# Layer 0's down projection: F tiles 16 to 21 of both token chunks by seven block products in place of eight

## The chip, the cores and the metric

The kernel runs on one core of a Trainium2 chip. The metric is the device time of one execution in microseconds (us), the median over several runs. The core's engines are TensorE (PE in the profile, its weight loads PEld), VectorE (DVE), ScalarE (ACT), GpSimd (POOL) and SyncE (SP). SP and POOL also issue the DMAs; each works off its queue in order.

## The reference

Two residual layers over 1024 tokens of width 1024, each a token mixer (layer 0 a causal convolution module, layer 1 a multi-scale pooling) and a SwiGLU network with 2816 hidden channels:

```python
def swiglu_ffn(h, w_gate, w_up, w_down):
    return (jax.nn.silu(h @ w_gate) * (h @ w_up)) @ w_down
...
for i in range(DEPTH):
    mod = c_act @ ada_w[i] + ada_b[i]
    sh_m, sc_m, g_m, sh_f, sc_f, g_f = jnp.split(mod, N_ADA, axis=-1)
    h = modulate(rms_norm(x, norm_mix_g[i]), sh_m, sc_m)
    y = conformer_conv(h, ...) if i % 2 == 0 else multiscale_pool(h, ...)
    x = x + (1.0 + g_m)[:, None, :] * y
    h = modulate(rms_norm(x, norm_ffn_g[i]), sh_f, sc_f)
    x = x + (1.0 + g_f)[:, None, :] * swiglu_ffn(h, ...)
return rms_norm(x, final_g)
```

The change is in `@ w_down` of layer 0: the hidden values g (2816 by 1024 tokens) times a 2816 by 1024 matrix.

## The kernel before

**Tiles.** Tokens are two chunks, A and B, of 512. Channels lie on the 128 partitions: 8 blocks d of the model width, 22 F tiles of the hidden width, two to a pair. A float32 operand is split into a high part (a copy on ScalarE, `hi` or the first half of `w`) and a low part (a subtraction on VectorE, `lo` or the second half). `products` (line 505) issues three 128x512 matmuls for each product of a weight tile and an operand: a row "x3" of PE's order is one product.

**Stages, in PE's order.** Layer 0's convolution; `heads` (gate and up of chunk A's first pairs, and their part of A's down); `joint` (gate and up of the rest for both chunks together, in fewer products by a block scheme on sums and differences); `downs` (line 1860), first of chunk A's remaining F tiles, then of all 22 of chunk B; then the same for layer 1. A gated tile g goes to DRAM (`gd`) and comes back when its down is due.

**Down** (`down`, line 1404). F tiles are taken in groups of up to four (`fours`); for each of eight output blocks d the group's products add up in one of the `dn` banks, and `update` (line 1021) has VectorE add the bank, times a gain, to `x`. A's 14 remaining tiles make four groups, B's 22 make six.

**Layer 1's down** already goes by `Seven` (line 1504): four F tiles are taken as a 2 by 2 block of matrices over the two halves of the output and the two tokens' chunks, and p1 to p7 (seven products of sums of weight blocks `wds` and of operands `kinds`, `kept`) replace eight. Each such product is added to up to two places of `x`, so its bank is read by VectorE once for each place, and p1, p6, p7, p4 go on adding to one set of four banks, with reads between. Weights are combined by a load that adds to a tile already loaded (`plus` in `weights_of`, line 1441: an SP load, then a POOL load with addition) and by subtraction on VectorE.

**The pool mixer of chunk A** (layer 1's first part) is done beside B's down of layer 0. `pool_start(A)` (line 1942) puts a task with VectorE's work in the planner's list: A's norm statistics (`acc`, a matmul `var` over 128 channels, eight small steps to the reciprocal root, a matmul `rstd` that spreads it), then `t`, the window sums `win` and their difference to the token, whose low parts are the rows `mx<-win`. `pool_end(A)` (line 1947) puts the mixer's 16 products (`y<-mx`, 48 matmuls), with the rest of the task ahead of them, at a place in PE's order.

**What sets the order.** PE's order is as the program emits it (`manual_schedule`, line 134). While it emits, `pace` (line 233) keeps a clock for each engine from the costs in `PRICES` (line 93) and lets the tasks on VectorE go ahead up to 4 us past PE's clock; a task that waits for another engine is held back for a `DELAY`. So where a row stands in VectorE's queue is decided by these planned clocks. VectorE works its queue strictly in order. Other work that it has here: low parts of weights (`w<-raw`), dot products of layer 1's conditioning (`adaw`, 128x1024, each with a 512 KB load on POOL's queue) and the updates (`x<-dn`).

Of the kernel before, what the change touches and what calls it, by code (L numbers as in the profile page):

```python
# [9 lines left out]
F32 = mybir.dt.float32  # L10
# [46 lines left out]
ON_DVE = (1, 4)  # L57
AHEAD = 4
RECENT = 6
STRASSEN = (False, True)  # L60
NQ = -(-NP // 2)
LAST = (2, 3, 4)
LOADED = 4
SPLIT = 2
# [67 lines left out]
def trunk(ctx, tc, xT, c, vec, ada, adan, w1f, w1, wdg, w2, wgu, wdn, wds, wpl, out):  # L132
# [72 lines left out]
    def nm(s):  # L205
        uid[0] += 1
        return f"{s}_{uid[0]}"
# [131 lines left out]
    rd = [[dram.tile([P, 2, 512], F32, name=f"rd_{l}_{f}") for f in range(NP)] for l in range(DEPTH)]  # L339


    kept_d = [[dram.tile([P, 2, 512], F32, name=f"kept_{l}_{q}") for q in range(NQ)] if STRASSEN[l] else [] for l in range(DEPTH)]
    kinds_d = [[[dram.tile([P, 2, 2, 512], F32, name=f"kinds_{l}_{q}_{b}") for b in range(3)] for q in range(NQ)] if STRASSEN[l] else [] for l in range(DEPTH)]
    KINDS = {"t1": (0, 0), "b22": (0, 1), "t3": (1, 0), "t2": (1, 1), "b11": (2, 0), "t4": (2, 1)}

    def x_out(ch):
# [693 lines left out]
    def gated(l, i, f, g, u, kept=False, into=None):  # L1040

        t = temp(512)
        S_.activation(t, g, AF.Silu)
        if into is not None:
            V_.tensor_tensor(into, u, t, op=MUL)
            return
        V_.tensor_tensor(t, u, t, op=MUL)
        if STRASSEN[l]:
            soft.dma_start(kept_d[l][f // 4][:, f // 2 % 2], t)
            if not kept:  # L1050
                return
        both = block("u0", "g")
        split(t, both, V_ if kept else None)
        if kept:
            st["g", i, f] = both[:, 0], both[:, 1]
        else:
            soft.dma_start(gd[l][i][f], both.bitcast(F32))
# [60 lines left out]
    def joint_weights(l, fp):  # L1118

        w = {}  # L1120

        def added(i, src):
            d = order(nc.gpsimd.dma_start(w[i], wgu[l, fp, src], accum_op=ADD))  # L1123
            if fp == 1:
                st["added"].append(d.ins)
            clock["G"] = max(clock["G"], clock["PE"]) + 0.9

        def loads():
            for i in (0, 3, 2, 1) if fp else (2, 0, 3, 1):
                w[i] = quarter(l, fp, i, "u1")  # L1130
            if fp == 2:
                V_.tensor_tensor(w[0], w[0], w[2], op=ADD)
            elif fp == 1 and l == 0:
                V_.tensor_tensor(w[0], w[0], w[2], op=ADD)
                if st["third"]:
                    tc.add_manual_dep(V_.last.ins, st["third"], edge, reason="behind the combinations")
                else:
                    st["early"].append(V_.last.ins)
            else:
                added(*((0, 2) if fp else (2, 3)))  # L1140
            added(*((2, 3) if fp else (0, 2)))

        def later():

            if fp == 1 and st["read"]:
                tc.add_manual_dep(V_.last.ins, st["read"], edge, reason="behind the first unit's reads")
            elif fp == 1:
                st["next"].append(V_.last.ins)

        def s2():  # L1150
            if fp:
                loads()
            w[4] = block("u0", "s2", F32).rearrange("p a b -> p (a b)")
            either(D).tensor_tensor(w[4], w[0], w[3], op=ADD)
            later()
            wt = combined(w[4])
            later()
            return wt

        def s1():  # L1160
            if fp == 0:
                loads()
            wt = combined(w[2], fp == 0)
            if fp:
                later()
            return wt

        def s3():
            wt = combined(w[0], fp == 0, True)
            later()  # L1170
            return wt

        def s4():
            either(D).tensor_tensor(w[1], w[1], w[4], op=ADD)
            if STRASSEN[l] and "taken" in st:
                tc.add_manual_dep(V_.last.ins, st["taken"], edge, reason="behind the second sum's banks")
            return combined(w[1])

        def a22():
            wt = combined(w[3], fp == 0 and l == 0, True, wgu[l, fp, 3])  # L1180
            if fp == 0 and l == 0:
                return wt
            if fp == 0 and st["third"]:
                tc.add_manual_dep(V_.last.ins, st["third"], edge, reason="behind the combinations")
            elif fp == 0:
                st["early"].append(V_.last.ins)
            return wt

        return s2, s1, s3, s4, a22

    def joint(l, fp, between=None):
# [29 lines left out]
        def after5(o, b):  # L1221
            if fp:
                r = temp(512)
            else:
                c["r15"] = c["r15"] if o else block("u0", "r15", F32)
                r = c["r15"][:, o]
            c["r15", o] = r
            V_.tensor_tensor(r, b, c["r1"][o], op=ADD)
            if STRASSEN[l] and o:
                st["taken"] = V_.last.ins.name  # L1230

        def ended(r, i, f, op):
            def after(o, b):
                t = c["r1"][o] if r == "r1" else c[r, o]
                V_.tensor_tensor(t, b, t, op=op)
                c["c", o] = t
                if fp == 0 and r == "r15" and o:
                    st["read"] = V_.last.ins.name
                    for ins in st["next"]:
                        tc.add_manual_dep(ins, st["read"], edge, reason="behind the first unit's reads")  # L1240
                if o and STRASSEN[l]:
                    paired(i, f, c["c", 0], t)
                elif o:
                    gated(l, i, f, c["c", 0], t)
            return after
# [195 lines left out]
    def weights_of(l, kind, q, placed=True):  # L1441

        n = duo_width(q) * 512
        src = lambda b: wds[q, b][:, :n]
        got = {}

        def behind_products(d):
            if placed:
                tc.add_manual_dep(d.ins, last_mm[0], held_by if kind == "s4" else edge, reason="behind the products")

        def plus(r, what):
            behind_products(nc.gpsimd.dma_start(r, what, accum_op=ADD))
            clock["G"] = max(clock["G"], clock["PE"]) + 0.9

        def load():
            if kind == "a11":
                st["sum", q] = block("h1", "s", F32).rearrange("p a b -> p (a b)")[:, :n]
            if kind in ("a11", "s2", "s4"):
                r = st["sum", q]
            else:  # L1460
                r = (raw_tile() if placed else raws.tile([P, D], F32, tag="raw", name=nm("raw")))[:, :n]
            first = {"a11": 0, "a12": 1, "a22": 3, "s1": 2, "s3": 3}.get(kind)
            if first is not None:
                behind_products(nc.sync.dma_start(r, src(first)))
            if kind in ("s1", "s4"):
                plus(r, src(3 if kind == "s1" else 1))
            got["raw"] = r

        def halves():
            r = got["raw"]  # L1470
            if kind == "s3":
                V_.tensor_tensor(r, r, st["sum", q], op=ADD)
            wt = wts.tile([P, 2, D], F32R, tag="w", name=nm("w"))
            S_.copy(wt[:, 0, :n], r)
            V_.tensor_tensor(wt[:, 1, :n], r, wt[:, 0, :n].bitcast(F32), op=SUB)
            if kind == "s1":
                st["then_sum"] = lambda: V_.tensor_tensor(st["sum", q], st["sum", q], r, op=SUB)
            return wt

        return load, halves  # L1480
# [85 lines left out]
    def one_half(l, qs):  # L1566
# [14 lines left out]
        bs = []  # L1581
        for q in qs:
            unit(emit_of(q, bs), lambda q=q: queued(weights_of(l, "a12", q, False)))

    def ending(ch, l):

# [284 lines left out]
    def heads(l, n, first):  # L1871

        for r in range(ROUNDS[l]):
            fps = range(r * ROUND, (r + 1) * ROUND)
            in_turn(l, fps, True)
            if r == 0:
                first()
            if STRASSEN[l]:
                one_half(l, [fps[0] // 2, fps[0] // 2 + 1])
            else:  # L1880
                down(A, l, [2 * q for q in fps])
# [7 lines left out]
    def all_joint(l, n, first=None, behind_it=None, between=None):  # L1889
# [3 lines left out]
        unit(lambda take: T.__setitem__("comb", Task(combinations(l, st["sq"]), True)))  # L1893
        in_turn(l, range(n, NP), behind_it=behind_it)
        need("comb")
        rest = [2 * q for q in range(ROUNDS[l] * ROUND, NP)] + list(range(1, NF, 2))
        for fp in range(NP):
            joint(l, fp, between if fp == NP - 1 else None)
            if 2 < fp <= 2 + KT // 2:
# [1 line left out]
            if fp == 0:  # L1901
                if first is not None:
                    first()
            if fp == NP - 2 and not STRASSEN[l]:
                unit(fetch(A, l, fours(rest)[0], "h1"))
        return rest

# [28 lines left out]
        for k in range(KT):  # L1936
            yield from pool_mixed(ch, k)

    downs(A, 0, rest, "h1", {0: lambda: unit(lambda take: x_in(B))}, True)
    unit(lambda take: lax.__setitem__(0, True))  # L1940

    def pool_start(ch):
# [13 lines left out]
        else:  # L1956
            unit(lambda take: st.__setitem__("sq", sq[0]))

    downs(B, 0, list(range(NF)), "h1", {0: lambda: pool_start(A), 4: lambda: pool_end(A)})
    need("norm_a")  # L1960
    pool_start(B)
    heads(1, HEADS[1], lambda: None)
# [88 lines left out]
```

## Time and profile before

| what | value |
|---|---|
| median of 3 runs | 1693.41 us (1692.5 to 1693.59) |
| the profiled execution | 1691.56 us, its span 1689.7 us |
| mean granted TensorE clock | 0.998 |
| PE busy | 1663.7 us, 98% of the span |
| DVE busy | 1318.1 us, 78% |
| ACT, POOL busy | 798.4 us (47%), 490.9 us (29%) |
| DMA | 380.71 MB, mean 225 GB/s |

Time outside the span is 1.86 us. PE is busy nearly all the time, so a matmul less is time saved unless PE is then made to wait; a wait of PE is time lost. Times in the views are microseconds from the start of the span. An instruction's duration overlaps the next one's on the same engine a little: how far apart instructions start is the better measure of what each costs in a row.

### The profile page before, as it was taken

Reading aid. Unit: us, or ns where it says so; the run is one execution under the profiler, and the core shown is the slowest. Engines: PE = TensorE matmul, PEld = TensorE weight load, DVE = VectorE, ACT = ScalarE, POOL = GpSimd, SP = SyncE. Lnnn points to the kernel's source line nnn. Section 1 sums busy time; section 2 is a strip of 40 time slices with the busy share of each in tenths; the row PEclk is TensorE's granted clock in tenths of the full one; section 3 lists DMA queues with packets and bytes.
Section 4 is the critical chain, followed back from the end, with each engine's and each line's share of the span. In section 5 each row is a group of like instructions: output and inputs, shape, how many; then the busy total and the mean of one; then the engine's idle time right before and its main releaser. Section 6 shows DMA issues by size and latency. Waiting matters only on the chain.

```text
span 1689.7 us, 21273 instructions
## 1 busy us (share of the span) xinstructions
PE 1663.7 (98%) x7586; PEld 1357.1 (80%) x7586; DVE 1318.1 (78%) x1872; ACT 798.4 (47%) x1085; POOL 490.9 (29%) x566
## 2 busy tenths in 40 slices
PE   6999999999999999999999999999999999999997
PEld 5777777778888888888888888888888888888887
DVE  8889899899759888887665797848777777668656
ACT  3669686867546332333213336646422222234344
POOL 3587767797001121221110221100111111000013
PEclk9999999999999999999999999999999999999999
DMA  7957997828677788886877846877677776577564
GB/s 288 296 181 221 226 240 209 225 77 237 206 243 177 257 262 300 280 268 208 338 267 269 262 147 201 241 244 212 178 231 218 225 220 192 205 268 208 191 168 125
DMA packets 115885, 380.71 MB, mean 225 GB/s; under 512 B 12289, under 2 KB 14465, under 8 KB 115778
## 3 DMA queue, kind: packets, MB, share of 16 engines
q1 hardware_dynamic: 78464, 247.99, 41.4%
q0 software_dynamic: 36736, 130.83, 31.7%
q8 instruction: 60, 0.98, 0.2%
q10 hardware_dynamic: 578, 0.53, 0.1%
q14 instruction: 47, 0.39, 0.1%
HBM read 311.92 MB, written 63.18 MB: 222 GB/s over the span
## 4 chain that ended last, share of the span: by engine, by line
PE 90%; DVE 4%; DMA 2%; issue 1%; POOL 1%; ACT 1%; SPq 0%; DVEq 0%; ACTq 0%; POOLq 0%
PE a L149 25%; PE dn L149 23%; PE e L149 14%; PE p L149 12%; PE y L149 6%; PE g L149 3%; PE first L149 3%; PE tap L149 2%; POOL pa L126 1%; PE ada L149 1%; DMA adaw<-in_adan_dram 1%; DVE t L126 1%; PE var L149 1%; DVE x L126 1%; DVE ca L126 0%
## 5 line engine op out<-in xcount | busy, mean ns | idle before, releaser
L126 ACT CAST w<-raw 128x1024 fp32r<-128x1024 f32 (+1 forms) x249 | 258.6, 1041 | 324.8 <-PE dn L149 92.1
L149 PE MATMUL dn<-g,w 128*128 128x512 f32 x1152 | 265.4, 391 | 1.7 <-DVE g L126 1.0
L149 PEld LDWEIGHTS dn<-g,w 128*128 128x128 f32 x1152 | 215.5, 188 | 48.0 <-DVE g L126 1.3
L126 DVE TENSOR_TENSOR w<-raw,w 128x1024 fp32r<-128x1024 f32 (+1 forms) x177 | 217.7, 1232 | 38.2 <-ACT w L126 37.8
L149 PE MATMUL a<-n,w 128*128 128x512 f32 x1056 | 246.9, 390 | 0.2
L149 PE MATMUL p<-h,w 128*128 128x512 f32 x1056 | 244.2, 391 | 0.8 <-DVE h L126 0.7
L126 POOL TENSOR_TENSOR pa<-pa,pr 128x512 f32<-128x512 f32 x160 | 228.2, 1510 | 23.7 <-ACT pr L126 17.5
L149 PEld LDWEIGHTS p<-h,w 128*128 128x128 f32 x1056 | 197.3, 188 | 43.8 <-DVE h L126 1.5
L149 PEld LDWEIGHTS a<-n,w 128*128 128x128 f32 x1056 | 198.2, 188 | 42.1 <-DVE r L126 1.1
L149 PE MATMUL dn<-hi,w 128*128 128x512 f32 (+1 forms) x600 | 173.9, 373 | 0.5 <-DVE w L126 0.5
L126 DVE SCALAR_TENSOR_TENSOR ca<-u,vecs,ca 128x512 f32<-128x512 f32 x245 | 169.6, 745 | 0.5
L126 DVE SCALAR_TENSOR_TENSOR x<-dn,gains,x 128x512 f32<-128x512 f32 (+1 forms) x144 | 100.7, 729 | 35.4 <-PE dn L149 35.1
L149 PEld LDWEIGHTS dn<-hi,w 128*128 128x128 f32 x600 | 109.8, 188 | 20.6 <-DVE w L126 1.0
L149 PE MATMUL a<-t,w 128*128 128x512 f32 x528 | 123.3, 389 | 0.0
L149 PE MATMUL e<-b,w 128*128 128x512 f32 x528 | 123.3, 389 | 0.0
L149 PE MATMUL e<-t,w 128*128 128x512 f32 x528 | 123.3, 389 | 0.0
L126 ACT ACTIVATE pr<-u,vecs 128x512 f32<-128x512 f32 x160 | 108.3, 717 | 25.3 <-POOL pa L126 17.6
L1123 POOL DMA_DIRECT2D raw<-in_wgu_dram x41 | 36.2, 882 | 275.2 <-DVE k L126 106.9
L149 PEld LDWEIGHTS a<-t,w 128*128 128x128 f32 x528 | 99.1, 188 | 20.6
L149 PEld LDWEIGHTS e<-b,w 128*128 128x128 f32 x528 | 99.1, 188 | 20.5
L149 PEld LDWEIGHTS e<-t,w 128*128 128x128 f32 x528 | 99.1, 188 | 20.5
L149 PE MATMUL dn<-lo,w 128*128 128x512 f32 (+1 forms) x300 | 111.7, 372 | 0.0
(183 smaller groups left out, 2376.1 us busy)
## 6 DMA issues: line engine op xcount, KB each, us to landing
raw<-in_wgu_dram SPq DMA_DIRECT2D x132, 512.0 KB, 4.8
adaw<-in_ada_dram POOLq DMA_DIRECT2D x48, 512.0 KB, 7.3
raw<-in_wdn_dram SPq DMA_DIRECT2D x44, 512.0 KB, 7.7
raw<-in_wgu_dram POOLq DMA_DIRECT2D x41, 512.0 KB, 7.5
raw<-in_w_dram SPq DMA_DIRECT2D x36, 512.0 KB, 5.7
gd<-g POOLq DMA_DIRECT2D x36, 512.0 KB, 8.2
g<-gd SPq DMA_DIRECT2D x36, 512.0 KB, 5.4
kinds<-k POOLq DMA_DIRECT2D x33, 512.0 KB, 7.3
```

The lines of the kernel that those rows point to most:

```text
L126: self.last = self.order(getattr(self.eng, name)(out, *args, **kw))
L149: last_mm[0] = nc.tensor.matmul(out, lhsT, rhs, start=start, stop=stop, skip_group_check=more).ins.name
L1123: d = order(nc.gpsimd.dma_start(w[i], wgu[l, fp, src], accum_op=ADD))
```

## The change

F tiles 16 to 21 of layer 0's down are taken by seven products, as `q=4` (tiles 16 to 19) and `q=5` (tiles 20 and 21, half the width). A's remaining tiles are then 8 (two groups), followed by p2, p1, p6, p7, p4, p5, p3, each for q=5 and q=4; p4 completes chunk A. Then come B's first 16 tiles (four groups in place of six). `pool_start(A)` moves behind p4, `pool_end(A)` behind the third of B's groups (before: started behind the first, ended behind the fifth). The hidden values of these tiles go to DRAM as sums (`kinds`, `kept`) and not as `gd`, weights combined in `weights_of` have an own way for layer 0 (s1 is loaded again by an SP and a POOL load, since `s2` comes first).

```diff
-STRASSEN = (False, True)
+BEGINS = (8, 0)
+BY_SEVEN = tuple(range(q, NQ) for q in (BEGINS[0] // 2, 0))
...
-        if STRASSEN[l]:
+        if f // 2 >= BEGINS[l]:
             soft.dma_start(kept_d[l][f // 4][:, f // 2 % 2], t)
...
-            if kind in ("a11", "s2", "s4"):
+            if kind in ("a11", "s2", "s4") and (l or kind != "s2"):
                 r = st["sum", q]
...
-            first = {"a11": 0, "a12": 1, "a22": 3, "s1": 2, "s3": 3}.get(kind)
+            first = {"a11": 0, "a12": 1, "a22": 3, "s1": 2, "s3": 3, **({} if l else {"s2": 2})}.get(kind)
             if first is not None:
                 behind_products(nc.sync.dma_start(r, src(first)))
-            if kind in ("s1", "s4"):
-                plus(r, src(3 if kind == "s1" else 1))
+            if kind in ("s1", "s4") or kind == "s2" and not l:
+                plus(r, src(1 if kind == "s4" else 3))
...
+            elif kind == "s2" and not l:
+                total = st["sum", q]
+                V_.tensor_tensor(total, total, r, op=SUB)
+                r = total
...
+    def seven_queued(l, steps, after):
+
+        todo = [(name, wkind, key, fresh, ends, q) for name, wkind, _, key, fresh, ends in steps for q in BY_SEVEN[l][::-1]]
+        parts = [operand(l, kind, q) for _, _, kind, *_ in steps for q in BY_SEVEN[l][::-1]]
+        last_q, counts, ready, banks = BY_SEVEN[l][0], [0, 0], {}, {}
+
+        def prepare(i):
+            while counts[0] < min(i + LOADED, len(parts)):
+                parts[counts[0]][0]()
+                counts[0] += 1
+            while counts[1] < min(i + SPLIT, len(parts)):
+                ready[counts[1]] = parts[counts[1]][1]()
+                counts[1] += 1
+
+        def emit_of(i, name, wkind, key, fresh, ends, q):
+            def emit(take):
+                wt = take()
+                prepare(i + 1)
+                if fresh and q != last_q:
+                    banks[key] = [bank("dn") for _ in range(4)]
+                bs, ops = banks[key], ready.pop(i)
+                for ds in ((0, 1), (2, 3)):
+                    for j, g in enumerate(ops):
+                        for d in ds:
+                            last = q == last_q and j == len(ops) - 1
+                            products(bs[d], wt, 4 * j + d, g, fresh and q != last_q and j == 0, last, more=True)
+                            if last:
+                                for ch, half in ends:
+                                    update(ch, 4 * half + d, bs[d], gate_f, l)
+                        pace()
+            return emit
...
-        rest = [2 * q for q in range(ROUNDS[l] * ROUND, NP)] + list(range(1, NF, 2))
+        rest = list(range(1, 2 * BEGINS[l], 2))
...
-    downs(B, 0, list(range(NF)), "h1", {0: lambda: pool_start(A), 4: lambda: pool_end(A)})
+    first_b = list(range(2 * BEGINS[0]))
+    begun.append(seven_queued(0, [
+        ("p2", "a12", "b21", "y", True, [(A, 0)]),
+        ("p1", "a11", "b11", "x", True, [(A, 0)]),
+        ("p6", "s2", "t2", "x", False, [(B, 0)]),
+        ("p7", "s3", "t3", "x", False, [(B, 1)]),
+        ("p4", "a22", "t4", "x", False, [(A, 1)]),
+        ("p5", "s1", "t1", "y", True, [(B, 1), (B, 0)]),
+        ("p3", "s4", "b22", "y", True, [(B, 0)]),
+    ], {"p4": lambda: pool_start(A), "p5": lambda: unit(fetch(B, 0, fours(first_b)[0], "h1"))}))
+    downs(B, 0, first_b, "h1", {2: lambda: pool_end(A)}, True)
```

Three places of the instruction order matter below. In an order row the numbers behind the names tell buffers apart. The first place is PE's queue around the pool norm and the pool mixer's products. Before, `var` is row 1318 and the first `y` row 1414, with 94 rows of `dn` and one of `rstd` between:

```order
L149 MATMUL dn_7890<-g_7670,w_7596 128x512 x3
L149 MATMUL dn_7891<-g_7670,w_7596 128x512 x3
L149 MATMUL var_7903<-ones,acc_7773 128x1 x4
L149 MATMUL dn_7890<-g_7672,w_7719 128x512 x3
L149 MATMUL dn_7891<-g_7672,w_7719 128x512 x3
...
L149 MATMUL dn_8416<-g_8223,w_8301 128x512 x3
L149 MATMUL dn_8417<-g_8223,w_8301 128x512 x3
L149 MATMUL y_8465<-mx_8025,w_8314 128x512 x3
L149 MATMUL y_8465<-mx_8033,w_8314 128x512 x3
```

In the changed kernel `var` is row 1492 and the first `y` row 1562, with 68 rows of `dn` and one of `rstd` between; the last pool tile, `mx_8451`, is first used in row 1575:

```order
L150 MATMUL dn_7961<-g_7818,w_7838 128x512 x3
L150 MATMUL dn_7962<-g_7818,w_7838 128x512 x3
L150 MATMUL dn_7989<-g_7812,w_7719 128x512 x3
L150 MATMUL dn_7990<-g_7812,w_7719 128x512 x3
L150 MATMUL dn_7989<-g_7814,w_7768 128x512 x3
L150 MATMUL dn_7990<-g_7814,w_7768 128x512 x3
L150 MATMUL var_8013<-ones,acc_7735 128x1 x4
L150 MATMUL dn_7989<-g_7816,w_7809 128x512 x3
...
L150 MATMUL dn_8397<-g_8172,w_8254 128x512 x3
L150 MATMUL y_8454<-mx_8124,w_8267 128x512 x3
...
L150 MATMUL y_8524<-mx_8451,w_8406 128x512 x3
```

So 26 products (78 matmuls) less stand between `var` and the first `y`: 204 `dn` matmuls in place of 282.

The second place is VectorE's queue at the end of the same stretch. Before, the row of the last low part (`mx_8351<-win`) stands ahead of the first update from `y`:

```order
L126 SCALAR_TENSOR_TENSOR win_8291<-win_8290,hp_7764 128x497
L126 SCALAR_TENSOR_TENSOR x_7217<-dn_8416,gains,x_7217 128x512
L126 SCALAR_TENSOR_TENSOR x_7217<-dn_8417,gains,x_7217 128x512
L126 TENSOR_TENSOR w_8449<-raw_8447,w_8449 128x1024
L126 TENSOR_TENSOR mx_8351<-win_8291,mx_8351 128x512
L126 SCALAR_TENSOR_TENSOR x_5638<-y_8465,gains,x_5638 128x512
```

In the changed kernel the last three low parts come behind updates that read the first `y` banks:

```order
L127 TENSOR_TENSOR mx_8326<-win_8306,mx_8326 128x512
L127 TENSOR_TENSOR win_8329<-win_8330 128x520
L127 TENSOR_TENSOR acc_8462<-acc_8462,t_8494 128x512
L127 TENSOR_TENSOR win_8385<-hp_7726 128x526
L127 TENSOR_TENSOR win_8330<-win_8329 128x512
L127 SCALAR_TENSOR_TENSOR x_6050<-y_8502,gains,x_6050 128x512
...
L127 TENSOR_TENSOR mx_8376<-win_8330,mx_8376 128x512
L127 TENSOR_TENSOR acc_8462<-acc_8462,t_8521 128x512
L127 TENSOR_TENSOR win_8386<-win_8385 128x512
L127 SCALAR_TENSOR_TENSOR win_8386<-win_8386,hp_7726 128x497
L127 TENSOR_TENSOR mx_8451<-win_8386,mx_8451 128x512
```

From the first row on `var` to the last low part these are 95 rows before and 97 in the changed kernel.

The third place is VectorE's queue in the seven products, which before has no counterpart. The banks `dn_7463` to `dn_7466` are those that p1, p6, p7 and p4 share; the updates of `x_7212` and `x_7214` read them behind p6, those of `x_7216` and `x_7218` behind p7; `raw_7611` is s1 of q=4 and `raw_7587` that of q=5:

```order
L127 SCALAR_TENSOR_TENSOR x_7212<-dn_7464,gains,x_7212 128x512
L127 SCALAR_TENSOR_TENSOR x_7214<-dn_7465,gains,x_7214 128x512
L127 SCALAR_TENSOR_TENSOR x_7214<-dn_7466,gains,x_7214 128x512
L127 TENSOR_TENSOR lo_7620<-op_7550,hi_7619 128x1024
L127 TENSOR_TENSOR w_7590<-raw_7587,w_7590 128x512
L127 TENSOR_TENSOR lo_7661<-op_7593,hi_7660 128x512
L127 SCALAR_TENSOR_TENSOR x_7216<-dn_7463,gains,x_7216 128x512
L127 SCALAR_TENSOR_TENSOR x_7216<-dn_7464,gains,x_7216 128x512
L127 SCALAR_TENSOR_TENSOR x_7218<-dn_7465,gains,x_7218 128x512
L127 TENSOR_TENSOR w_7614<-raw_7611,w_7614 128x1024
L127 SCALAR_TENSOR_TENSOR x_7218<-dn_7466,gains,x_7218 128x512
```

The low part of s1's weights now stands ahead of the last of the updates that p4's products wait for.

More of the change, by code (lines that the diff above doesn't have):

```diff
@@ L339, in trunk @@
     rd = [[dram.tile([P, 2, 512], F32, name=f"rd_{l}_{f}") for f in range(NP)] for l in range(DEPTH)]
-    kept_d = [[dram.tile([P, 2, 512], F32, name=f"kept_{l}_{q}") for q in range(NQ)] if STRASSEN[l] else [] for l in range(DEPTH)]
-    kinds_d = [[[dram.tile([P, 2, 2, 512], F32, name=f"kinds_{l}_{q}_{b}") for b in range(3)] for q in range(NQ)] if STRASSEN[l] else [] for l in range(DEPTH)]
+    kept_d = [{q: dram.tile([P, 2, 512], F32, name=f"kept_{l}_{q}") for q in BY_SEVEN[l]} for l in range(DEPTH)]
+    kinds_d = [{q: [dram.tile([P, 2, 2, 512], F32, name=f"kinds_{l}_{q}_{b}") for b in range(3)] for q in BY_SEVEN[l]} for l in range(DEPTH)]
     KINDS = {"t1": (0, 0), "b22": (0, 1), "t3": (1, 0), "t2": (1, 1), "b11": (2, 0), "t4": (2, 1)}
@@ L1174, in s4 @@
             either(D).tensor_tensor(w[1], w[1], w[4], op=ADD)
-            if STRASSEN[l] and "taken" in st:
+            if fp >= BEGINS[l] and "taken" in st:
                 tc.add_manual_dep(V_.last.ins, st["taken"], edge, reason="behind the second sum's banks")
@@ L1228, in after5 @@
             V_.tensor_tensor(r, b, c["r1"][o], op=ADD)
-            if STRASSEN[l] and o:
+            if fp >= BEGINS[l] and o:
                 st["taken"] = V_.last.ins.name
@@ L1240, in after @@
                         tc.add_manual_dep(ins, st["read"], edge, reason="behind the first unit's reads")
-                if o and STRASSEN[l]:
+                if o and fp >= BEGINS[l]:
                     paired(i, f, c["c", 0], t)
@@ L1443, in weights_of @@
         n = duo_width(q) * 512
-        src = lambda b: wds[q, b][:, :n]
+        src = lambda b: wds[l, q, b][:, :n]
         got = {}
@@ L1475, in halves @@
             V_.tensor_tensor(wt[:, 1, :n], r, wt[:, 0, :n].bitcast(F32), op=SUB)
-            if kind == "s1":
+            if kind == "s1" and l:
                 st["then_sum"] = lambda: V_.tensor_tensor(st["sum", q], st["sum", q], r, op=SUB)
@@ L1583, in one_half @@
             unit(emit_of(q, bs), lambda q=q: queued(weights_of(l, "a12", q, False)))
+    def seven_queued(l, steps, after):
[26 more added lines that the diff above has]
+            return emit
+        for i, (name, wkind, key, fresh, ends, q) in enumerate(todo):
+            unit(emit_of(i, name, wkind, key, fresh, ends, q), lambda wkind=wkind, q=q: queued(weights_of(l, wkind, q, False)))
+            if name in after and q == last_q:
+                after[name]()
+        return lambda take: prepare(0)
     def ending(ch, l):
@@ L1877, in heads @@
                 first()
-            if STRASSEN[l]:
+            if not BEGINS[l]:
                 one_half(l, [fps[0] // 2, fps[0] // 2 + 1])
@@ L1903, in all_joint @@
                     first()
-            if fp == NP - 2 and not STRASSEN[l]:
+            if fp == NP - 2 and BEGINS[l]:
                 unit(fetch(A, l, fours(rest)[0], "h1"))
@@ L1937, in pool @@
             yield from pool_mixed(ch, k)
-    downs(A, 0, rest, "h1", {0: lambda: unit(lambda take: x_in(B))}, True)
+    begun = []
+    downs(A, 0, rest, "h1", {0: lambda: (unit(lambda take: x_in(B)), unit(lambda take: begun[0](take)))}, True)
     unit(lambda take: lax.__setitem__(0, True))
@@ L2018 @@
             diag[i, range(P), q, range(P)] = taps[j, p]
-    down = np.asarray(ffn_w_down)[1].reshape(NP, 2, P, 2, D // 2)
-    pairs = np.zeros((NQ, 4, P, 2, D // 2), np.float32)
+    down = np.asarray(ffn_w_down).reshape(DEPTH, NP, 2, P, 2, D // 2)
+    pairs = np.zeros((DEPTH, NQ, 4, P, 2, D // 2), np.float32)
     for q in range(NP):
         for b, (f, half) in enumerate(((1, 0), (0, 0), (1, 1), (0, 1))):
-            pairs[q // 2, b, :, q % 2] = down[q, f, :, half]
-    pairs = pairs.reshape(NQ, 4, P, D)
+            pairs[:, q // 2, b, :, q % 2] = down[:, q, f, :, half]
+    pairs = pairs.reshape(DEPTH, NQ, 4, P, D)
     arrays = {
```

## The prediction

> **What bounds the kernel now.** I read the page first (span, busy time of the engines, chain), then PE's waits, then PE's timeline from the last `joint` products to layer 1's gate, then the windows of that stretch, VectorE's timeline in it and the DMA issues.
>
> ```profile
> span 1689.7 us, 21273 instructions
> PE 1663.7 (98%) x7586; PEld 1357.1 (80%) x7586; DVE 1318.1 (78%) x1872; ACT 798.4 (47%) x1085; POOL 490.9 (29%) x566
> PE 90%; DVE 4%; DMA 2%; issue 1%; POOL 1%; ACT 1%; SPq 0%; DVEq 0%; ACTq 0%; POOLq 0%
> ```
>
> PE is the bound: 98% busy and 90% of the chain. Its waits (kind, total, times, longest) are small:
>
> ```profile
> PE var L149 <- DVE acc L126: 6.5, 1, 6.5
> ...
> PE dn L149 <- DVE g L126: 1.0, 1, 1.0
> ```
>
> The 6.5 us are at the start of the program; no `dn` group of waits is over 1.0 us. So every matmul taken out is time saved, as long as nobody makes PE wait. PE's timeline (start, length, operation, count, idle time before it) around the change:
>
> ```profile
> 811.45 5.60 PE L149 MATMUL e<-b,w 128*128 128x512 f32 x24
> 816.88 5.60 PE L149 MATMUL a<-n,w 128*128 128x512 f32 x24
> 822.33 115.76 PE L149 MATMUL dn<-g,w 128*128 128x512 f32 x510
> 937.92 0.95 PE L149 MATMUL var<-ones,acc 128*128 128x1 f32 x8
> 938.73 4.33 PE L149 MATMUL dn<-g,w 128*128 128x512 f32 x18
> 942.90 0.60 PE L157 MATMUL rstd<-ident,col 128*128 128x128 f32 x4
> 943.26 18.63 PE L149 MATMUL dn<-g,w 128*128 128x512 f32 x81
> 962.14 42.05 PE L149 MATMUL dn<-g,w 128*128 128x512 f32 x183 [0.25 <-DVE x L126]
> 1004.03 11.04 PE L149 MATMUL y<-mx,w 128*128 128x512 f32 x48
> 1014.91 5.60 PE L149 MATMUL dn<-g,w 128*128 128x512 f32 x24
> ```
>
> From 822 to 1015 PE waits once, for 0.25 us. A matmul costs (816.88 - 811.45) / 24, or 0.226 us; over the 48 `y` it is 10.88 / 48 = 0.2267, which I use. VectorE is the other full engine there (window, then its length, PE, PEld, DVE, ACT, POOL busy with counts, clock, DMA share, GB/s):
>
> ```profile
> 822.30:862.00 39.70, 39.70 (x177) 32.87 (x176) 26.18 (x36) 9.06 (x9) 3.98 (x8) 1.00 0.79 297
> 938.00:1004.00 66.00, 65.75 (x295) 53.89 (x294) 59.95 (x95) 25.85 (x33) 19.16 (x30) 1.00 0.65 215
> ```
>
> Beside the pool mixer VectorE is busy 59.95 of 66 us. That is the narrow place.
>
> **Part 1: matmuls removed.** By the instruction order PE has 36 128x512 matmuls less (six F tiles by two chunks by eight blocks are 96 products; seven eighths are 84, so 12 x 3 matmuls go) and no other change of kind. All stand in the dense stretch: 36 x 0.2267 = 8.2 us saved.
>
> **Part 2: the seven products' own stage.** It is 252 matmuls (57 us). One set of banks is read by VectorE and added to again four times in a row, so each product waits for the updates of the one before. VectorE's costs, by the distance between starts:
>
> ```profile
> 938.91 0.16 DVE L126 TENSOR_SCALAR col<-var 128x4 int32<-128x4 int32 x1 [1.39 <-PE var L149]
> 939.11 0.17 DVE L126 TENSOR_TENSOR var<-var,col 128x4 f32<-128x4 f32 x1
> ...
> 940.42 1.23 DVE L126 TENSOR_TENSOR w<-raw,w 128x1024 fp32r<-128x1024 f32 x1
> 941.57 1.22 DVE L126 SCALAR_TENSOR_TENSOR adaw<-adaw,cact 128x1024 f32<-128x1024 f32 x1
> 942.71 0.08 DVE L126 DVE_READ_ACCUMULATOR adaw<-adaw,cact 128x1 f32 x1
> ...
> 950.76 0.68 DVE L126 TENSOR_TENSOR win<-hp 128x512 f32<-128x512 f32 x1
> 951.36 0.74 DVE L126 SCALAR_TENSOR_TENSOR t<-x,gains,ny 128x512 f32<-128x512 f32 x1
> 952.02 0.68 DVE L126 TENSOR_TENSOR win<-hp 128x512 f32<-128x512 f32 x1
> ```
>
> So 1.14 us for 1024 elements (`w`, `adaw`), 0.66 for an update or `t`, 0.60 for other rows of 512, 0.20 for the small steps. The narrow place is s1's weights, which now take two loads one behind the other, SP's and then POOL's adding one (in layer 1's down: landing times):
>
> ```profile
> raw<-in_wds_dram SPq DMA_DIRECT2D x10, 512.0 KB, 7.1
> raw<-in_wds_dram POOLq DMA_DIRECT2D x5, 512.0 KB, 8.1
> ...
> raw<-in_wds_dram SPq DMA_DIRECT2D x5, 512.0 KB, 5.1
> s<-in_wds_dram POOLq DMA_DIRECT2D x5, 512.0 KB, 5.2
> ```
>
> ```profile
> L126 ACT CAST w<-raw 128x1024 fp32r<-128x1024 f32 (+1 forms) x249 | 258.6, 1041 | 324.8 <-PE dn L149 92.1
> L1123 POOL DMA_DIRECT2D raw<-in_wgu_dram x41 | 36.2, 882 | 275.2 <-DVE k L126 106.9
> ```
>
> The SP load reuses a buffer that VectorE frees when it has split a22. That is behind the last of p1's updates: matmul 72 of the stage (16.3 us), an update (0.7), then four rows (1.14 + 1.14 + 1.14 + 0.60), 21.1 us. The chain adds 5.1 to 7.1 (SP), 0.9 (POOL's issue), 5.2 to 8.1 (POOL), 1.04 (ScalarE's copy) and 1.14 (low part): 34.5 to 39.4, and 0.66 for the update queued behind it, 35.2 to 40.1. The fourth bank's product of p4, which needs that update, comes at matmul 153, 34.7 us. PE waits 0.5 to 5.4 us; I take 3, the middle, since the rows come from two stretches with about equal claim. Queued behind: on ScalarE the casts of p5's and p3's operands, on SP B's second weight tile, which has 20 us more before PE needs it; on POOL the clearing of the pool's borders and the first `wdn` load. None of these is due before p4. The operand splits (7 of 1.14, 7 of 0.60) and the subtractions for s2, s3 lie beside 57 us of products, and B's updates are no more than before.
>
> **Part 3: the pool mixer of A.** It moves into a shorter piece of PE's queue. Between `var` and the first `y` stood 282 `dn` matmuls, 66.1 us (937.92 to 1004.03). Now 204 stand there: 204 x 0.2267 + 0.81 + 0.36 for `var` and `rstd` = 47.4 us. The product that needs the last low part of `mx` is 39 matmuls and the first of its three behind `y`, 9.1 us: 75.2 us before, 56.5 now.
>
> VectorE's rows in the same piece do not shrink. Before, its timeline ends the piece so:
>
> ```profile
> 973.52 1.23 DVE L126 SCALAR_TENSOR_TENSOR adaw<-adaw,cact 128x1024 f32<-128x1024 f32 x1 [4.90 <-DMA adaw<-in_ada_dram]
> ...
> 1008.34 0.68 DVE L126 TENSOR_TENSOR mx<-win,mx 128x512 fp32r<-128x512 f32 x1
> ```
>
> 938.91 to 1009.02 is 70.1 us, of which 4.9 was a wait for a dot's data: 65.2 us of work in 95 rows. The same costs applied to these 95 rows (8 small, 17 wide, 34 updates and `t`, 36 others) give 1.6 + 19.4 + 22.4 + 21.7 = 65.1: the ledger holds. Now 97 rows: 8 small, 16 wide, 32 updates and `t`, 41 others: 1.6 + 18.2 + 21.1 + 24.8 = 65.7 us. Eight updates of `dn` went; six of `y` and five sums of its squares came in ahead of the last low part. From `var` that part is ready after 1.0 (937.92 to 938.91) + 65.7 = 66.7 us without a wait, and PE wants it after 56.5. PE waits 10.2 us, or 15.1 with a wait for data such as the 4.9 of before. I take 12.5, between them, since the six dots and ten weights of the piece are again loaded beside it. The 4 us of slack that this place had (1009.02 against 1013.1) is gone.
>
> Nothing gives it back: behind `y` PE is the bound again (B's last group has four tiles where it had three, so the norm that follows is not later than before).
>
> **Sum.** -8.2 + 3 + 12.5 = +7.3 us. The profiled execution took 1691.56 (span 1689.7 and 1.86 around it), so the same execution would take 1698.9. The median is 1693.41, 1.85 above it: 1700.7. With the low ends (-8.2 + 0.5 + 10.2 = +2.5) 1695.9, with the high ones (-8.2 + 5.4 + 15.1 = +12.3) 1705.7.
>
> **The rivals.** *VectorE keeps up (faster).* Place: the `y` products of the last pool group. For it: the order is made by planned clocks that left slack there before, and PE waits nowhere in this stage now. If the low part is ready 56.5 us after `var`, part 3 is nothing: -8.2 + 3 = -5.2, 1688.2 us. It decides at 12.5 - 5.2, so once VectorE gains more than 7.3 us on my ledger the kernel isn't slower; at 6 us gained it is 1693.41 + 7.3 - 6 = 1694.7. Against: the ledger gave before's piece within 0.1 us. Full form 0.10, half form 0.08.
>
> *The DMAs run full in the seven products' stage (slower still).* The share was already 0.79 in that stretch. For loads of the dots a later window has:
>
> ```profile
> adaw<-in_ada_dram POOLq DMA_DIRECT2D x4, 512.0 KB, 9.7
> ```
>
> With 9.7 for both of s1's loads the wait is 5.4 + 2.6 + 1.6 = 9.6: -8.2 + 9.6 + 12.5 = +13.9, 1707.3 us. Against: s2's and s3's loads start early. 0.11.
>
> *The clock falls in the gap.* PE's waits at `y` come in two pieces, one before the third low part from the end (some 5 us) and one before the last. The granted clock behind PE's waits:
>
> ```profile
> 13.19 1.86 PE L149 MATMUL var<-ones,acc 128*128 128x1 f32 x8 [6.46 <-DVE acc L126]
> ```
>
> ```profile
> 14.00:18.00 4.00, 2.15 (x10) 2.10 (x11) 3.68 (x14) 1.04 (x1) 0.00 (x0) 1.00 1.02 410
> 1685.00:1690.00 5.00, 0.00 (x0) 0.00 (x0) 0.61 (x2) 0.00 (x0) 0.00 (x0) 0.50 0.59 202
> ```
>
> Behind a wait of 6.46 us the clock stood at 1.00; with PE idle at the end it fell to 0.50. If it falls to 0.50 and stays there as long as a gap of 5 us, 2.5 us are added: +9.8, 1703.2 us. 0.13.
>
> The Trainium skill (TensorE: Matmul & The Clock Gate, section "Part 1: The HAM clock gate") says that an idle window of about 3.4 us halves the clock until about 3.4 us of work have passed, which would make it 1.7 us. The end of the trace agrees with the fall, the row at 13.19 doesn't show it.
>
> That the change saves no matmuls is ruled out by the order.
>
> **How the numbers follow.** My forecast has 0.58, and its own range (1695.9 to 1705.7) dips below 1696.8 with 0.10 of that. 0.2% (3.4 us) is about what a measurement can tell from no change. Faster by more (under 1690.0): 0.10. Within: 0.08 + 0.10 = 0.18. Slower: 0.48 + 0.11 + 0.13 = 0.72. The range leaves out the full form of the first rival below and about half of the DMA rival above: 1693 to 1707.5.
>
> **What would show it.** Right: in the changed trace PE's waits list `y` on DVE `mx` with 10 to 15 us; the last `mx` low part ends about 67 to 72 us behind `var`; PE waits for DVE `x` in the seven products by 0.5 to 5 us. Part 1 is wrong if `dn` matmuls no longer follow at 0.2267 us. The forecast is wrong if `y` starts 47 us behind `var` and the 48 `y` take their 11 us, which would say that VectorE's rows were not in the way.

## The result and the profile after

The changed kernel takes 1710.82 us (median of 4 runs, 1710.23 to 1711.78) against 1692.95 us (4 runs): 17.9 us slower, a ratio of 1.0105 with a 95% interval of 1.0093 to 1.0118. The direction is the one forecast, the size is not: 1700.7 was predicted and 1707.5 was the upper end of the range. The profiled execution took 1710.44 us, its span 1708.7. Of all the executions used below one is left out of its median: a run of the kernel with the early `var` that took 5587.72 us.

The page of the changed kernel (span, busy time, chain):

```profile
span 1708.7 us, 21245 instructions
PE 1665.1 (97%) x7550; PEld 1354.9 (79%) x7550; DVE 1335.0 (78%) x1894; ACT 800.3 (47%) x1087; POOL 488.9 (29%) x570
PE 85%; DVE 5%; DMA 4%; issue 3%; POOL 1%; ACT 1%; SPq 0%; DVEq 0%; POOLq 0%; ACTq 0%
```

PE has 36 instructions less and yet is busy for longer (1665.1 against 1663.7 us), a first sign that matmuls ran slower somewhere. Its share of the chain fell from 90 to 85%; DMA's rose from 2 to 4%. PE's waits, where before no `dn` kind was over 1.0 us and no pool `y` stood in the list:

```profile
PE dn L150 <- DVE x L127: 8.5, 5, 3.3
...
PE y L150 <- ACT mx L127: 5.7, 3, 3.4
...
PE y L150 <- DVE mx L127: 2.8, 2, 1.6
```

These are the two places that the prediction named: the shared banks of the seven products, and the pool mixer. PE's timeline, the starts behind which PE had to wait (four in the seven products), then the pool norm and the mixer:

```profile
883.30 0.47 PE L150 MATMUL dn<-hi,w 128*128 128x512 f32 x1 [0.97 <-DVE x L127]
892.83 0.47 PE L150 MATMUL dn<-hi,w 128*128 128x512 f32 x1 [1.13 <-DVE x L127]
903.70 0.47 PE L150 MATMUL dn<-hi,w 128*128 128x512 f32 x1 [2.43 <-DVE x L127]
909.30 0.79 PE L150 MATMUL dn<-hi,w 128*128 128x512 f32 x1 [3.32 <-DVE x L127]
```

```profile
952.24 0.95 PE L150 MATMUL var<-ones,acc 128*128 128x1 f32 x8
...
974.11 26.84 PE L150 MATMUL dn<-g,w 128*128 128x512 f32 x117 [0.62 <-DVE x L127]
1000.78 1.52 PE L150 MATMUL y<-mx,w 128*128 128x512 f32 x6
```

```profile
1010.48 0.51 PE L150 MATMUL y<-mx,w 128*128 128x512 f32 x1 [3.42 <-ACT mx L127]
1012.20 3.78 PE L150 MATMUL y<-mx,w 128*128 128x512 f32 x8 [1.21 <-DVE mx L127]
1016.58 0.80 PE L150 MATMUL y<-mx,w 128*128 128x512 f32 x1 [0.60 <-ACT mx L127]
1018.96 1.22 PE L150 MATMUL y<-mx,w 128*128 128x512 f32 x2 [1.58 <-DVE mx L127]
1021.90 4.51 PE L150 MATMUL y<-mx,w 128*128 128x512 f32 x9 [1.72 <-ACT mx L127]
1026.21 6.58 PE L150 MATMUL dn<-g,w 128*128 128x512 f32 x24
```

The 48 `y` matmuls took 11 us before; now they stretch from 1000.78 to 1026.21, 25.4 us. Only 8.5 us of that are waits. The last nine matmuls from 1021.90 wait for nothing more and take 4.3 us where 2.0 are due. The windows say why (clock is the third figure from the right):

```profile
865.84:933.20 67.36, 59.52 (x254) 47.98 (x252) 53.21 (x72) 24.01 (x31) 8.47 (x20) 0.97 0.78 237
```

```profile
1010.00:1020.00 10.00, 6.12 (x12) 3.46 (x12) 10.00 (x17) 2.31 (x4) 0.44 (x2) 0.56 0.16 63
1020.00:1030.00 10.00, 8.28 (x23) 6.16 (x23) 4.36 (x7) 2.82 (x4) 2.43 (x10) 0.59 0.13 52
```

The granted clock is 0.56 and 0.59 there, and VectorE is busy for all of the first window: it is what PE waits for, in three of the five waits by way of ScalarE's copies (`ACT mx`) of what VectorE has just written. The 17.5 us by which layer 1's first `p` starts later (1050.31 against 1032.84) come out as follows, each part against its count of matmuls at 0.2267 us:

| part | us |
|---|---|
| 36 matmuls less | -8.2 |
| seven products: 67.4 us (865.84 to 933.20) for 252 matmuls, 57.1 | +10.2 |
| `var` to the first `y`: 48.5 where 47.4 were due | +1.1 |
| `y`: 25.4 in place of 10.9 | +14.5 |
| the 24 `dn` behind it: 6.4 in place of 5.4 | +1.0 |
| the piece of before was itself 1.0 longer than by count (66.1 for 65.1) | -1.0 |
| sum | +17.6 |

What holds the seven products, in the chain that ended last (start, length, what):

```profile
889.19 7.69 DMA raw<-in_wds_dram
...
897.55 8.63 DMA raw<-in_wds_dram
...
906.28 1.05 ACT w L127
...
908.50 0.76 DVE x L127
...
909.30 5.70 PE dn L150 x18
```

That is the chain of the prediction: s1's two loads, ScalarE's copy, the low part (907.36 to 908.5 on VectorE), the update behind it, PE; but with loads of 7.7 and 8.6 us.

### The profile page after: what moved, and what is told of

Its sections match the earlier page's. It is cut to its first block, busy times and chain, and to the rows that moved or that the text cites. A ratio compares the mean times of both kernels' runs of the same rounds, so it can differ in the third digit from the quotient of the medians.

```text
span 1708.7 us, 21245 instructions
## 1 busy us (share of the span) xinstructions
PE 1665.1 (97%) x7550; PEld 1354.9 (79%) x7550; DVE 1335.0 (78%) x1894; ACT 800.3 (47%) x1087; POOL 488.9 (29%) x570
## 4 chain that ended last, share of the span: by engine, by line
PE 85%; DVE 5%; DMA 4%; issue 3%; POOL 1%; ACT 1%; SPq 0%; DVEq 0%; POOLq 0%; ACTq 0%
PE a L150 24%; PE dn L150 19%; PE e L150 14%; PE p L150 12%; PE y L150 6%; PE g L150 3%; PE first L150 3%; PE tap L150 2%; DMA raw<-in_wds_dram 2%; POOL pa L127 1%; PE ada L150 1%; DVE x L127 1%; DMA adaw<-in_adan_dram 1%; DVE win L127 1%; DVE w L127 1%
## 5 line engine op out<-in xcount | busy, mean ns | idle before, releaser
L127 ACT CAST w<-raw 128x1024 fp32r<-128x1024 f32 (+1 forms) x245 | 253.0, 1034 | 326.1 <-PE dn L150 75.9
L127 DVE TENSOR_TENSOR w<-raw,w 128x1024 fp32r<-128x1024 f32 (+1 forms) x175 | 213.0, 1222 | 42.1 <-ACT w L127 41.9
L150 PE MATMUL dn<-hi,w 128*128 128x512 f32 (+1 forms) x768 | 228.0, 379 | 8.8 <-DVE x L127 7.8
L150 PE MATMUL dn<-g,w 128*128 128x512 f32 x864 | 201.0, 392 | 2.0 <-DVE g L127 1.0
L150 PEld LDWEIGHTS dn<-g,w 128*128 128x128 f32 x864 | 162.5, 189 | 37.1 <-DVE g L127 1.3
L150 PEld LDWEIGHTS dn<-hi,w 128*128 128x128 f32 x768 | 142.1, 189 | 37.4 <-issue 4.2
L150 PE MATMUL dn<-lo,w 128*128 128x512 f32 (+1 forms) x384 | 145.1, 378 | 0.0
L127 ACT ACTIVATE pr<-u,vecs 128x512 f32<-128x512 f32 x160 | 108.3, 717 | 25.3 <-POOL pa L127 17.9
```

The costliest lines, as they stand in the source:

```text
L127: self.last = self.order(getattr(self.eng, name)(out, *args, **kw))
L150: last_mm[0] = nc.tensor.matmul(out, lhsT, rhs, start=start, stop=stop, skip_group_check=more).ins.name
```

## The experiments

All changes below are to the changed kernel, but for one that is to the kernel before. Times are medians. The kernel before was measured again beside them: 1691.87 us beside the runs without the adding load, with the kept sum, with the later start and with the filler, 1692.55 us beside the other four, against 1692.95 beside the changed kernel. So a gain over the changed kernel's 1710.82 can be up to 1.1 us too large.

**s1 without its adding load.**

```diff
-            if kind in ("s1", "s4") or kind == "s2" and not l:
+            if kind == "s1" and l or kind == "s4" or kind == "s2" and not l:
                 plus(r, src(1 if kind == "s4" else 3))
```

> The changed kernel with the second (adding, POOL) load of s1's weights left out in layer 0, so that p5 is computed with one weight block in place of the sum of two. Theory (a chain of two loads holds p4's updates): the two last waits of the seven products' stage, 2.4 and 3.3 us, and the slow clock behind them go: 6 to 8 us less than the changed kernel's 1710.8, 1703 to 1705. Rival (VectorE cannot turn the shared banks round in time, whatever the weights do): within 2 us of 1710.8.

The kernel computes p5 with one weight block in place of the sum of two. Measured: 1702.85 us, 8.0 less than the changed kernel (6.9 if each is taken against the kernel before beside it). PE's waits in the stage are now

```profile
876.17 0.50 PE L150 MATMUL dn<-hi,w 128*128 128x512 f32 x1 [1.21 <-DVE x L127]
883.98 0.47 PE L150 MATMUL dn<-hi,w 128*128 128x512 f32 x1 [1.36 <-DVE x L127]
893.51 0.47 PE L150 MATMUL dn<-hi,w 128*128 128x512 f32 x1 [1.10 <-DVE x L127]
```

The two long ones are gone, and with them the slow clock; the theory holds. Three waits of some 1.2 us stay.

**s1's sum kept** from s2 on in a tile of its own (slots that are free until the pool mixer's inputs come), not loaded again.

```diff
+            if kind == "s1" and not l:
+                got["raw"] = st["sum_s1", q]
+                return
...
+            elif kind == "s2":
+                r = st["sum_s1", q] = block("u0", "raw", F32).rearrange("p a b -> p (a b)")[:, :n]
```

> The changed kernel with s1's sum kept in a tile of its own from s2 on, so that neither of its two loads is done again. Theory: the same two waits go, 6 to 8 us less than 1710.8, about 1703 to 1705, the same as without the adding load. Rival one (banks turned round too slowly): within 2 us of 1710.8. Rival two (the DMAs are simply full, so every load counts): at least 3 us lower than the run without the adding load, since twice as many loads are gone.

Measured: 1699.07 us, 11.7 less. The theory's 1703 to 1705 is missed: the time is 3.8 below the run before it, as the second rival asked, so by these two alone the number of loads could be what counts. The next one separates that.

**s2's sum in its own tile, s1 with its base load alone.**

```diff
+            elif kind == "s2":
+                r = block("u0", "raw", F32).rearrange("p a b -> p (a b)")[:, :n]
...
-            if kind in ("s1", "s4") or kind == "s2" and not l:
+            if kind == "s1" and l or kind == "s4" or kind == "s2" and not l:
```

> The run without the adding load of s1 (1702.9), with s2's sum moreover in a tile of its own, out of the three buffers that the other weights' loads take in turn; s1's base load stays. As there, p5 is computed with one block in place of the sum of two. It tells why keeping the sum gave 3.8 us more: by buffers that come free sooner (then about 1699), or by the two base loads that are not made (then 1702 to 1704).

Measured: 1699.54 us. The base loads are back and the time is that of the kept sum: the 3.8 us come with the tile that leaves the buffers which the weights' loads take in turn, not from the loads' number. In the changed kernel VectorE waited for a weight block's load ahead of PE's first wait in the stage:

```profile
874.07 0.69 DVE L127 TENSOR_TENSOR raw<-raw,s 128x512 f32<-128x512 f32 x1 [1.98 <-DMA raw<-in_wds_dram]
```

With s2 out of the three buffers its timeline has no such wait: SP issues this load (s3 of q=5) at 845.91 and not at 864.30. The edit also moves rows in VectorE's queue (this subtraction comes ahead of a dot product and of two low parts), and no run separates the two. The stage's length by PE's timeline, from its first matmul to B's first:

| kernel | from, to | us |
|---|---|---|
| changed | 865.84, 933.20 | 67.4 |
| s1 without its adding load | 864.60, 926.29 | 61.7 |
| and s2 in its own tile | 864.87, 923.79 | 58.9 |
| s1's sum kept | 864.73, 922.98 | 58.3 |
| 252 matmuls at 0.2267 | | 57.1 |

So of the 10.2 us lost here about 5.7 are the adding load's and 2.8 the buffers' (with the rows that move), and 1.1 stay. These are single traces: with the same rows in this stage the runs with the filler and with the earlier products below took 69.4 and 68.8 us for it, so each share is good to some 2 us, and the 0.7 between the last two kernels can't be told from nothing.

**The kernel before with the mixer's start one group later.**

```diff
-    downs(B, 0, list(range(NF)), "h1", {0: lambda: pool_start(A), 4: lambda: pool_end(A)})
+    downs(B, 0, list(range(NF)), "h1", {1: lambda: pool_start(A), 4: lambda: pool_end(A)})
```

> The kernel before, without the seven products, with the pool mixer's start moved behind the second of B's groups in place of the first. PE then has 198 matmuls between var and the first product of y (204 in the changed kernel, 282 before), VectorE the 97 rows of the changed kernel, 65.8 us. Theory (VectorE's rows in too short a piece of PE's queue): PE waits 66.8 - 55.2 = 11.6 us at y and 2 to 3 more for data, and the clock falls behind it, 3 us: 12 to 17 us slower than before, 1705 to 1710. Rival (the wait at y comes from the seven products, by lateness or by their DMAs): within 3 us of 1693.

Measured: 1705.17 us against 1691.87, 13.3 slower, ratio 1.0079 (1.0064 to 1.0094). Its timeline:

```profile
957.12 0.95 PE L149 MATMUL var<-ones,acc 128*128 128x1 f32 x8
...
1003.37 5.83 PE L149 MATMUL y<-mx,w 128*128 128x512 f32 x25
1011.11 1.18 PE L149 MATMUL y<-mx,w 128*128 128x512 f32 x2 [1.92 <-DVE mx L126]
...
1028.75 5.64 PE L149 MATMUL dn<-g,w 128*128 128x512 f32 x24
```

Without any of the seven products `y` takes 25.4 us again, from 1003.37 to 1028.75. A shorter piece of PE's queue beside the same work of VectorE is enough for this loss.

**The mixer's products one group earlier.**

```diff
-    downs(B, 0, first_b, "h1", {2: lambda: pool_end(A)}, True)
+    downs(B, 0, first_b, "h1", {1: lambda: pool_end(A)}, True)
```

> The changed kernel with the pool mixer's products put behind the second of B's groups in place of the third, 96 matmuls earlier. VectorE's rows from var to the last low part shrink from 65.8 to 57.1 us, PE's work to the product that needs it from 56.5 to 34.8 us. Theory (VectorE's rows against PE's piece): the wait grows from 12.7 to 23 to 26 us, so 11 to 14 us over the changed kernel, 1722 to 1725. Rival (the wait at y has a length of its own, data or a copy that comes late): within 3 us of 1710.8.

Measured: 1720.47 us, 9.7 more than the changed kernel and 1.5 under the range given. `y` starts at 979.57 and the next `dn` at 1017.90: 38.3 us, 13 more than the changed kernel's 25.4, as expected of `y`. The whole execution gained less: the profiled one took 1722.29 us, 11.9 more than the changed kernel's profiled one, and it was the slowest of its four. So the wait has no length of its own; where the rest of the 13 us went was not followed.

**Work in place of waiting.**

```diff
+    def filler(take):
+        b, (g, _) = bank("dn"), st["g", B.i, first_b[-1]]
+        for i in range(52):
+            matmul(b, g[:, :P], g, start=i == 0, stop=i == 51)
...
+        need(("pool", A.i))
+        unit(filler)
+        pool_end(A)
...
```

> The changed kernel with 52 matmuls on data that is there already, 11.8 us of work for nothing, ahead of the first y, so that PE works where it would wait. Theory (the clock falls in the gaps, which costs 3.4 us beyond the waiting): the granted clock stays at 1.00 through y, the filler takes the place of the wait of 12.7 us, and the kernel is 3 to 4.5 us faster than 1710.8, about 1707. Rival (the clock is no cost of its own): no faster, and slower by the part of the 11.8 us that isn't covered.

Measured: 1706.9 us, 3.9 less than the changed kernel (this run's interval against before is 1.0072 to 1.0102, that of the changed kernel 1.0093 to 1.0118, so the two just overlap). The timeline and the window behind it:

```profile
1002.96 11.95 PE L150 MATMUL dn<-g 128*128 128x512 f32 x52
1014.74 11.04 PE L150 MATMUL y<-mx,w 128*128 128x512 f32 x48
```

```profile
1014.00:1026.00 12.00, 12.00 (x54) 9.93 (x54) 11.36 (x19) 6.25 (x10) 2.02 (x10) 1.00 0.09 36
```

52 matmuls for nothing ahead of them, and `y` takes its 11.04 us without a wait at a clock of 1.00. But this run does not isolate the clock: three of `y`'s updates, in place of six and five sums of squares, now stand ahead of the last low part, which ends 65.4 us behind `var` and not 70.3. From `var` to the next norm's `var` the profiled execution takes 76.1 us in place of 80.4. Of these 4.3 us, 3.3 are what the last nine `y` and the 24 `dn` took beyond their count in the changed kernel, which its timeline shows by itself.

**`var` earlier.** The planner holds a norm's `var` back until 8 us past the clocks of VectorE and ScalarE (`DELAY_BEHIND`); here, for the pool norm of A alone, it may come 8 us ahead of them (the same line makes a second delay, `spread`, 3 us in place of 4).

```diff
-                    self.until = (self.mark + V_.spent if self.urgent else max(clock["V"], clock["S"])) + (DELAY if self.urgent or not lax[0] else DELAY_BEHIND)[said]
+                    self.until = (self.mark + V_.spent if self.urgent else max(clock["V"], clock["S"])) + (DELAY if self.urgent or not lax[0] else {"stats": -8, "spread": 3.0} if st.get("soon") and said in ("stats", "spread") else DELAY_BEHIND)[said]
...
```

> The changed kernel with the planner's delay between the last sum of squares and the matmul var taken out for this norm alone: var stands 16 rows (48 matmuls, 10.9 us) earlier in PE's order, the y products where they were; VectorE has 99 rows, 67.3 us, up to the last low part. Theory: the wait at y shrinks from 12.7 to between 1 and 4 us and the slow clock behind it goes: 9 to 14 us less than 1710.8, 1697 to 1702. Rival (var placed earlier only makes PE wait there, since the sums aren't ready): within 3 us of 1710.8.

Measured: 1696.33 us over nine executions, 14.5 less and 0.7 below the range given.

```profile
937.20 0.95 PE L150 MATMUL var<-ones,acc 128*128 128x1 f32 x8
...
995.68 9.00 PE L150 MATMUL y<-mx,w 128*128 128x512 f32 x39
1005.63 0.50 PE L150 MATMUL y<-mx,w 128*128 128x512 f32 x1 [0.95 <-ACT mx L127]
1007.45 3.60 PE L150 MATMUL y<-mx,w 128*128 128x512 f32 x8 [1.31 <-DVE mx L127]
1010.89 5.61 PE L150 MATMUL dn<-g,w 128*128 128x512 f32 x24
```

`var` did not wait: the sums were ready. From `var` to `y` are 58.5 us in place of 48.5, and `y` takes 15.2 us, not 25.4. Not all of the gain is `y`'s: in this trace the seven products take 64.0 us (865.01 to 929.04) in place of 67.4, with one dot product less in VectorE's queue there (889.05 in the changed kernel) and with s1's loads landed in 7.4 and 6.7 us.

**Both remedies.** The kept sum and the early `var` in one kernel.

> Both remedies: s1's sum kept, and var 16 rows earlier. Theory (the two waits are all that the seven products lost, and they add up): 1699.1 less 9 to 14 us, 1685 to 1690, so that the 8.2 us of matmuls saved show and the kernel beats the one before (1692) by 2 to 7 us. Rival (taking one wait away makes the other longer): not below 1692.

Measured: 1688.59 us (11 runs) against 1692.55 (21), ratio 0.9976, interval 0.9967 to 0.9985. It beats both kernels, by 4.0 and 22.2 us. The two gains alone were 11.7 and 14.5, 26.2 together, so they add up but for 4.0 us; the 3.3 us that the early `var` alone gained in the seven products fit most of that, since the kept sum takes the same loss away. What is left of waits (seven products, then `y`):

```profile
884.00 0.47 PE L150 MATMUL dn<-hi,w 128*128 128x512 f32 x1 [0.61 <-DVE x L127]
892.81 0.47 PE L150 MATMUL dn<-hi,w 128*128 128x512 f32 x1 [0.38 <-DVE x L127]
1001.94 0.49 PE L150 MATMUL y<-mx,w 128*128 128x512 f32 x1 [0.71 <-ACT mx L127]
1003.76 3.28 PE L150 MATMUL y<-mx,w 128*128 128x512 f32 x8 [1.32 <-DVE mx L127]
```

## Why the prediction was right or wrong

**Part 1 was right.** `dn` matmuls follow one another at 0.2267 us as before, and with the two waits mostly gone the kernel is 4.0 us faster than the one before.

**Part 2 was mis-sized, and is most of the miss: 3 us taken, 10.2 measured.** The mechanism was the one described, down to the update behind s1's low part. What failed is the step "I take 3, the middle, since the rows come from two stretches with about equal claim". They had no equal claim. The DMA share was 0.88 in the first of these stretches (1500 to 1550 of the kernel before) and 0.62 in the second (1600 to 1650). The stretch that runs into the seven products has a DMA share of 0.93 in the changed kernel, and the one in which s1's loads run 0.96 (the second figure from the right):

```profile
822.32:865.80 43.48, 43.48 (x193) 36.05 (x192) 29.46 (x41) 9.63 (x11) 6.61 (x11) 1.00 0.93 333
...
890.00:900.00 10.00, 8.87 (x40) 7.05 (x39) 5.79 (x9) 1.04 (x1) 2.75 (x11) 1.00 0.96 297
```

The loads of s1 landed in 7.7 and 8.6 us, beyond the slower of my rows; the half-width block's adding load in 10.4:

```profile
raw<-in_wds_dram POOLq DMA_DIRECT2D x1, 512.0 KB, 8.6
...
raw<-in_wds_dram POOLq DMA_DIRECT2D x1, 256.0 KB, 10.4
```

The half-width block's update held PE first (2.43 us), the full one's then (3.32): 5.75 us together, above the upper end of 5.4. The other 4.5 us weren't in the term at all. The first two waits, 0.97 and 1.13 us, come from three buffers that the weights' loads share, where s2's extra tile made the next load wait (with s2 in its own tile they are 0.61 and 0.66). Some 1.4 us are the slow clock (below), and 1.0 are small gaps that were not split further. The DMA rival had the right place, but it asked for loads of 9.7 us; that its 9.6 us lie near the 10.2 is luck.

**Part 3 was right in how late PE comes, and its own sign was missed.** PE was to come 12.5 us late at the product that needs the last low part. Without a wait it was due 47.4 + 8.8 us behind `var`, at 1008.5; it came at 1021.90, 13.4 late. The last low part starts on VectorE

```profile
1021.88 0.69 DVE L127 TENSOR_TENSOR mx<-win,mx 128x512 fp32r<-128x512 f32 x1 [1.06 <-ACT mx L127]
```

and so ends 70.3 us behind `var`, in the 67 to 72 given. VectorE's rows in it took 66.2 us where 65.7 were counted (41 rows at 0.60 are 24.6 and not 24.8, which changes nothing); its waits were 2.05 us for a dot's data and 1.06 for ScalarE's copy of the last tile, which itself waited for GpSimd's edge of that window (a `win` row at 1020.98). The sign, 10 to 15 us of waits on DVE `mx`, did not come: the list has 2.8 there and 5.7 on ACT `mx`, 8.5 in five pieces, since the 12 matmuls between the pieces ran at half the clock and took 3.8 us more than by count. The kernel before with a shorter piece, which shares nothing else with the change, lost 13.3 us in the same way.

**The clock rival came true beside the forecast, not in its place.** From 1021.90 on, with the last wait over, `y` and the 24 `dn` took 2.3 and 1.0 us too long: 3.3 where 2.5 was priced; and some 1.4 us in the seven products (8 matmuls from 909.30 to 912.55 are 3.25 us, 1.8 are due). The prediction read the row at 13.19 as a clock of 1.00 behind 6.46 us of idle time; but its eight `var` took 1.86 us where those at 937.92 took 0.95, so they ran at about half speed though the window's figure says 1.00, and the row is no case of a clock that held. The Trainium skill's rule (TensorE: Matmul & The Clock Gate, section "Part 1: The HAM clock gate"), an idle window of about 3.4 us halves the clock, fits this trace: behind 2.43 us idle the clock held, behind 3.32 and 3.42 it fell to 0.50. Its other half, that about 3.4 us of work bring the clock back, fits the seven products (3 us) and not the mixer (6 us, below). As a rule for the length of one wait it does not hold, though. With the early `var` alone 2.13 us were enough:

```profile
901.65 0.77 PE L150 MATMUL dn<-hi,w 128*128 128x512 f32 x1 [2.13 <-DVE x L127]
902.21 0.63 PE L150 MATMUL dn<-lo,w 128*128 128x512 f32 x1
```

The same rows took 0.47 and 0.39 us at full clock. The rule speaks of a window and not of a wait, and where its windows begin no run here shows.

**The range failed because the rivals were priced as exclusive.** Each shared its cause with the forecast: a longer wait for s1 and a halved clock can only come on top of the waits that I forecast. Taken together, by my own prices -8.2 + 9.6 + 12.5 + 2.5 is +16.4 us, 1709.8 by the median that I started from; the measured time is 1710.8. That sum is made after the result, and it is so close in part by luck, as the 9.6 stood for loads longer than those that came.

**VectorE keeping up** did not happen by itself, but the point that it decides was right: with `var` 16 rows earlier PE's waits at `y` shrink from 8.5 to 2.3 us.

## What to carry to other kernels

When work is taken off the engine that sets the time, count what must still be done beside what is left: the piece of PE's queue that the mixer hid in lost 78 matmuls, while VectorE's rows in it stayed at 66 us. Where a prediction has a wait of several microseconds in it, a falling clock and slower loads belong in its own upper end, not among the alternatives. A moved stage can need its delays tuned anew: 16 rows in PE's order and a tile kept turned 17.9 us lost into 4.0 gained.

## What the runs showed of the hardware

- After a first wait of 3.42 us, waits of 0.6 to 1.7 us with a few matmuls between kept the granted clock at 0.50 for about 16 us (windows of 2 us from 1012 to 1028), and it came back 6 us after the last wait. In the seven products, behind a single wait of 3.32 us with PE busy from then on, it was back after 3 us (0.50 from 909 to 912, 0.94 from 912 to 913).
- The length of a single wait did not decide whether the clock fell: 2.43 us left it at 1.00 (changed kernel, ending at 903.70); 2.13 us halved it (early `var`, ending at 901.65), and so did 0.71 and 1.32 us with one matmul between (both remedies, ending at 1003.76: 0.69 from 1004 to 1005, 0.50 from 1005 to 1007).
- A 256 KB adding load took 10.4 us beside others, longer than a 512 KB one a few microseconds later (8.6).
